# Scale part of the first mixer in column quarters between the key weights, shift part behind the query weights, dense weights packed in load order

## The chip, the core and the metric

The kernel runs on one core of one Trainium2 chip. The core has five engines with a queue of their own each: PE (TensorE: matmuls; PEld are its weight loads), DVE (VectorE), ACT (ScalarE), POOL (GpSimd) and SP, which only issues DMAs here; 16 DMA engines move data between HBM and SBUF. Each engine works through its queue in order and waits on semaphores. The metric is the device time of one execution in microseconds, less is better.

## The reference

One sequence of 256 rows of 1024, in float32. Two blocks; the first is the one that is changed:

```python
def first_block(x, c, w_in, w_out, sinks, rel_bias, w_ada, b_ada, norm_gains, w1, b1, w2, b2):
    c_act = jax.nn.silu(c)
    mod = c_act @ w_ada + b_ada                       # 1024 -> 6 x 1024
    sh1, sc1, g1, sh2, sc2, g2 = jnp.split(mod, 6, axis=-1)
    h = rmsnorm(x, norm_gains[0]) * (1.0 + sc1) + sh1
    y = token_mixer(h, w_in, w_out, sinks, bias_hb)   # h @ w_in -> qa, ka, va, qb, kb, vb
    x = x + g1 * rmsnorm(y, norm_gains[1])
    h = rmsnorm(x, norm_gains[2]) * (1.0 + sc2) + sh2
    y = jnp.square(jax.nn.relu(h @ w1 + b1)) @ w2 + b2
    return x + g2 * rmsnorm(y, norm_gains[3])
```

The mixer has 8 heads of block attention (qa, ka, va: 512 columns each) and 8 of windowed attention (qb; kb and vb of 128 columns). The second block has another mixer (mLSTM and differential attention) and a mixture of 16 experts, whose weights are most of the 511 MB that are read.

## The kernel before

Dense weights come through `Weights`. `unit` registers a load, in load order; `pump` issues the next one from SP (`dma_start` at L145) as soon as the arena (`wa` of 8 chunks of 1 MiB, `wb` of 2, `wc` of 1) has a free window; `done` frees a unit when all its readers have been issued. SP waits in order, so a load that waits for its space holds the later ones. `slice` names a part of a unit that `take` turns into two halves: a rounded high part (ACT cast, L224) and the rest as low part (DVE subtraction, L225), up to `LOOK` = 2 slices ahead. A float32 product is three matmuls, high x high, low x high and high x low (`mm3`, L304 to L306). The experts' rows come through `load_run`, into the same arenas once the dense weights have left them.

The kernel is one program; the order in which its Python emits instructions is, engine by engine, the order of the queues (`behind("x")` puts what it encloses after the instruction x). It begins with a warm-up of PE (L450), the sums of squares of X, and `sc`, silu(c) spread over 32 columns. The modulation vector is not a matmul of one row: `quarter_step` (L482) multiplies `sc` with 256 rows of a 1024-column part of `w_ada`, four matmuls of 512 columns in four groups of 32 PE columns, into one PSUM bank; after the fourth quarter `summed` (L488, L489) copies the bank and `quarter_cols` (L495, L497) sums the groups while it turns the row into a column vector `modT`, and adds the bias. That is done for the scale part (`sc0` to `sc3`), and then, between the keys, for the shift part (`sh0` to `sh3`).

X is scaled by the reciprocal of its row norm (`xn`: L695 on ACT, L696 on DVE; `rs` comes from POOL) and transposed by PE (L700) into `xT` (L703, L705). `A1` (L723, 8 columns) is the gain times one plus the scale. `key_operands` (L734 on) takes a slice of `ka` (256 rows) and makes the high and low parts of xT times A1 (`hsh` L737, `hsl` L738); `keys` (L747) multiplies. The keys are computed without the shift, whose contribution, one number a column, is added later: `shift_row` (L811) multiplies modT with the key weights, `shift_cols` (L821) turns the row, and `bk` is added when the keys leave PSUM (L856). The queries have the shift as two extra columns of `hs` instead (L772, L773; 258 columns). L762 is a small matmul that makes the distance biases (`bdist`, L764), which go out to DRAM and come back spread out as `tb`. `scaled` (L656 to L658) then makes the full normed rows `hTh`, `hTl` for the values (`va`), the second heads and so on; `acc` (L518, L520) sums a later part of `w_ada` on DVE.

Of the kernel before, what the change touches and what calls it, by code (L numbers as in the profile page):

```python
# [16 lines left out]
D = 1024  # L17
# [21 lines left out]
class Weights:  # L39
# [87 lines left out]
    def pump(self):  # L127
        while self.next < len(self.units):
            name, src, shape, row = self.units[self.next]
            n = math.prod(shape[1:])  # L130
            if row is not None:
                if not self.load_run(src, row, shape, n):
                    return
                continue
# [119 lines left out]
def block_kernel(ctx: ExitStack, tc: tile.TileContext, x, c, w_in, w_out, sinks, rel_bias, w_ada, b_ada,  # L254
                 norm_gains, w1, b1, w2, b2, norm_mix_g, w_in2, b_mgate, conv_w, conv_b, mlstm_g,
                 diff_lam, diff_g, w_up_a, w_up_b, w_out2, norm_ffn_g, w_router, w_gate_e, w_up_e,
                 w_down_e, norm_f_g, pos_hot, head_sel, out, dbg=None):
    nc = tc.nc
# [51 lines left out]
    wa = w_ada[0].rearrange("(k p) f -> p k f", p=128)  # L310
    wi = w_in[0].rearrange("(k p) f -> p k f", p=128)
    wo = w_out[0].rearrange("(k p) f -> p k f", p=128)
    w1v = w1[0].rearrange("(k p) f -> p k f", p=128)
    w2v = w2[0].rearrange("(k p) f -> p k f", p=128)
    wi2 = w_in2[0].rearrange("(k p) f -> p k f", p=128)
    wua = w_up_a[0].rearrange("(k p) f -> p k f", p=128)
    wub = w_up_b[0].rearrange("(k p) f -> p k f", p=128)
    wo2 = w_out2[0].rearrange("(k p) f -> p k f", p=128)

    def half_units(name, c0, n=2, of=None):  # L320
        w = 8 // n
        for i in of or range(n):
            W.unit(f"{name}{i}", wa[:, w * i:w * i + w, c0:c0 + 1024], [128, w, 1024], 1)

    def fm_unit(name, src, c0, n, readers=0):
        W.unit(name, src[:, :, c0:c0 + n], [128, 8, n], readers)
# [3 lines left out]
    def tm_unit(name, src, c0, n, readers=0):  # L330
        W.unit(name, src[:, :, c0:c0 + n], [128, 8, n], readers)
# [3 lines left out]
    def row_unit(name, src, k0):  # L335
        W.unit(name, src[:, k0:k0 + 4, :], [128, 4, 1024], 0)
        for k in range(4):
            W.slice(name, lambda t, k=k: t[:, k, :], [128, 1024])

    half_units("sc", 1024, 4)  # L340
    for i in range(2):
        W.unit(f"ka{i}", wi[:, 4 * i:4 * i + 4, 512:1024], [128, 4, 512], 1)
        for k in range(2):
            W.slice(f"ka{i}", lambda t, k=k: t[:, 2 * k:2 * k + 2, :], [128, 2, 512])
    W.mark("ka")
    half_units("sh", 0, 4)
    fm_unit("qa", wi, 0, 512)
    tm_unit("va", wi, 1024, 512)
    W.unit("kvb", wi[:, :, 2048:2304], [128, 8, 256], 0)
# [3 lines left out]
    W.unit("qb", wi[:, :, 1536:2048], [128, 8, 512], 0)  # L353
# [8 lines left out]
    row_unit("wo0", wo, 0)  # L362
    W.mark("wo0")
    row_unit("wo1", wo, 4)
    W.mark("w_out")
    tm_unit("w1_0", w1v, 0, 512, 1)
    W.mark("w1_0")
    for g in range(9):
        if 0 < g < 8:
            fm_unit(f"w1_{g}", w1v, g * 512, 512)  # L370
        if g > 0:
            row_unit(f"w2_{g - 1}", w2v, 4 * (g - 1))
# [3 lines left out]
    tm_unit("mv", wi2, 1024, 512)  # L376
    W.mark("mv")
    fm_unit("mk", wi2, 512, 512)
    fm_unit("mq", wi2, 0, 512)
    W.unit("mg", wi2[:, :, 2048:2064], [128, 8, 16], 1)  # L380
    tm_unit("mo", wi2, 1536, 512)
    fm_unit("dk", wi2, 2576, 512)
    fm_unit("dq", wi2, 2064, 512)
    tm_unit("dv", wi2, 3088, 512)
    for g in range(4):
        fm_unit(f"gt{g}", wi2, 3600 + g * 512, 512)
    W.mark("proj2")
    W.unit("wua", wua, [128, 4, 1024], 0)
    W.unit("wub", wub, [128, 4, 1024], 0)
# [3 lines left out]
    row_unit("wp0", wo2, 0)  # L393
    row_unit("wp1", wo2, 4)
# [15 lines left out]
    for i in range(2):  # L410
        W.unit(f"eh{i}", wde[E - 1][:, 12:16, 512 * i:512 * i + 512], [128, 4, 512], 1)
# [15 lines left out]
    hsh = sp.tile([128, 8, HW], F32R, name="hsh")  # L427
# [46 lines left out]
    def quarter_step(name, i, ps):  # L474


        t = W.raw(f"{name}{i}")
        for kk in range(2):
            k = 2 * i + kk
            for j in range(2):  # L480
                b = 64 * kk + 32 * j
                LAST["sums"] = mm(ps[b:b + 32, :], sc[:, k, :], t[:, kk, j * 512:(j + 1) * 512],  # L482
                                  start=(k < 2), stop=(k >= 6))
        W.done(f"{name}{i}")

# [196 lines left out]
    xn = big.tile([128, 2, D], F32, name="xn", tag="hTh")  # L682
# [1191 lines left out]
```

## Time and profile before

| | |
|---|---|
| three runs | 1462.71, 1465.15, 1467.64 us; median 1465.15 |
| profiled execution | 1463.22 us, its span 1461.4 us |
| PE busy | 1108.9 us (76%) |
| DVE, ACT, POOL busy | 468.4, 308.4, 156.9 us |
| HBM read | 511.41 MB, 351 GB/s over the span |
| mean DMA | 64526 packets; 46658 under 8 KB |

Busy shares are means over stages that differ: a front of some 24 us until the first key matmul, the dense stage up to about 558 us, and the experts to the end. So the rows below are read by stretch. In a timeline a row has the start, the time from the first start to the last end of such instructions in a row, the engine, the line, the operation, what is written from what, and in brackets the idle time ahead of it with what ended it. A matmul of float32 leaves two records.

### The profile page before, as it was taken

What the parts mean: (1) busy time and instruction counts of PE and PEld (TensorE: products, weight loads), DVE (VectorE), ACT (ScalarE), POOL (GpSimd) and SP (SyncE); (2) the same over time, 40 slices, a digit from 0 to 9 for tenths busy, and PEclk for the clock granted to TensorE, in tenths of its full rate; (3) what the DMA queues carried; (4) which work ended last, traced back from release to release, by engine and by line L of the source; (5) the groups of instructions that cost most, each with busy time, mean ns of one, the idle gap of its engine ahead of it and who ended that gap; (6) DMA issues with size and microseconds to landing.
All of it is one profiled execution on the core that took longest, in us unless ns stands there. A gap on an engine that the chain in (4) does not pass through costs nothing.

```text
span 1461.4 us, 16948 instructions
## 1 busy us (share of the span) xinstructions
PE 1108.9 (76%) x7140; PEld 623.7 (43%) x7140; DVE 468.4 (32%) x974; ACT 308.4 (21%) x547; POOL 156.9 (11%) x187
## 2 busy tenths in 40 slices
PE   7999999999999999857654665565656655665665
PEld 5777798988998994212111111111111111111112
DVE  4788657767888764101000010010000100001001
ACT  4555544454745541000000000000000000000001
POOL 1100534323022240000000000000000000000000
PEclk9999999999999999887788787888687879778788
DMA  9996356634438578999999999999999999999996
GB/s 365 379 345 255 121 188 248 242 138 156 150 116 317 198 322 365 430 429 432 429 430 431 430 430 432 430 430 429 430 430 428 428 433 431 431 430 429 429 430 260
DMA packets 64526, 513.58 MB, mean 351 GB/s; under 512 B 6022, under 2 KB 7239, under 8 KB 46658
## 3 DMA queue, kind: packets, MB, share of 16 engines
q1 hardware_dynamic: 62898, 508.54, 84.5%
q0 software_dynamic: 1408, 3.70, 0.8%
q8 instruction: 56, 0.92, 0.3%
q10 hardware_dynamic: 144, 0.26, 0.0%
q14 instruction: 20, 0.16, 0.0%
HBM read 511.41 MB, written 1.07 MB: 351 GB/s over the span
## 4 chain that ended last, share of the span: by engine, by line
DMA 54%; PE 40%; DVE 3%; POOL 1%; issue 1%; ACT 1%; SPq 0%; DVEq 0%; ACTq 0%; POOLq 0%
DMA we<-in_w_gate_e_dram 17%; DMA we<-in_w_up_e_dram 16%; DMA we<-in_w_down_e_dram 16%; PE tp L1683 5%; PE f L304 4%; PE f L306 4%; PE f L305 4%; PE big L304 3%; PE big L306 3%; PE big L305 3%; PE f L1701 3%; DMA wd<-in_w_down_e_dram 2%; DMA wa<-in_w_ada_dram 2%; PE tp L304 1%; PE tp L305 1%
## 5 line engine op out<-in xcount | busy, mean ns | idle before, releaser
L1683 PE MATMUL tp<-wa,work 128*32 128x512 f32 x1000 | 148.0, 745 | 102.6 <-DMA wa<-in_w_up_e_dram 79.8
L1691 DVE TENSOR_TENSOR work<-work,tp 128x512 f32<-128x512 f32 x16 | 11.0, 687 | 557.8 <-PE tp L1683 557.8
L225 DVE TENSOR_TENSOR wboth<-wa,wboth 128x1024 fp32r<-128x1024 f32 x116 | 143.8, 1246 | 44.6 <-ACT wboth L224 44.5
L224 ACT CAST wboth<-wa 128x1024 fp32r<-128x1024 f32 x116 | 120.7, 1046 | 134.6 <-PE f L306 52.5
L1683 PE MATMUL tp<-wd,work 128*32 128x512 f32 x568 | 93.1, 803 | 65.5 <-DMA wd<-in_w_gate_e_dram 36.2
L1701 PE MATMUL f<-wa,work 128*32 128x512 f32 (+1 forms) x504 | 81.6, 796 | 59.4 <-DMA wa<-in_w_down_e_dram 56.3
L1683 PEld LDWEIGHTS tp<-wa,work 128*32 128x32 f32 x1000 | 35.4, 132 | 213.2 <-DMA wa<-in_w_up_e_dram 94.1
L304 PE MATMUL f<-hTh,wboth 128*128 128x256 f32 (+1 forms) x416 | 119.4, 287 | 0.0
L1765 ACT ACTIVATE work<-f,gi 128x512 f32<-128x512 f32 x15 | 10.3, 687 | 516.5 <-PE f L1701 516.5
L306 PE MATMUL f<-hTh,wboth 128*128 128x256 f32 (+1 forms) x416 | 118.2, 284 | 0.0
L305 PE MATMUL f<-hTl,wboth 128*128 128x256 f32 (+1 forms) x416 | 117.9, 283 | 0.0
L1694 POOL TENSOR_SCALAR work<-iot,gi 128x256 f32<-128x256 f32 x16 | 14.8, 922 | 816.7 <-PE big L1769 804.7
L1766 DVE TENSOR_SCALAR work<-f,gi 128x512 f32<-128x512 f32 x15 | 11.3, 751 | 249.9 <-PE f L1701 249.9
L1683 PE MATMUL tp<-we,work 128*32 128x512 f32 x384 | 61.8, 793 | 36.2 <-DMA we<-in_w_gate_e_dram 24.9
L1683 PEld LDWEIGHTS tp<-wd,work 128*32 128x32 f32 x568 | 21.9, 143 | 135.7 <-issue 55.4
L304 PEld LDWEIGHTS f<-hTh,wboth 128*128 128x128 f32 x416 | 79.1, 190 | 1.0 <-issue 0.5
L305 PEld LDWEIGHTS f<-hTl,wboth 128*128 128x128 f32 x416 | 79.3, 191 | 0.4 <-issue 0.3
L306 PEld LDWEIGHTS f<-hTh,wboth 128*128 128x128 f32 x416 | 79.1, 190 | 0.2 <-issue 0.2
L1690 ACT ACTIVATE work<-tp 128x512 f32<-128x512 f32 x16 | 9.6, 597 | 294.6 <-PE tp L1683 294.6
L1701 PE MATMUL f<-wd,work 128*32 128x512 f32 x264 | 51.1, 859 | 26.9 <-DMA wd<-in_w_down_e_dram 26.9
L1701 PEld LDWEIGHTS f<-wa,work 128*32 128x32 f32 x504 | 22.3, 142 | 111.7 <-issue 107.6
L1769 PE MATMUL big<-work 128*128 128x512 f32 x120 | 55.1, 602 | 4.7 <-ACT work L1765 4.2
(539 smaller groups left out, 1884.1 us busy)
## 6 DMA issues: line engine op xcount, KB each, us to landing
wa<-in_w_up_e_dram SPq DMA_DIRECT2D x15, 4096.0 KB
wa<-in_w_down_e_dram SPq DMA_DIRECT2D x14, 4096.0 KB
wa<-in_w_gate_e_dram SPq DMA_DIRECT2D x14, 4096.0 KB
wa<-in_w_in_dram SPq DMA_DIRECT2D x14, 2048.0 KB
wd<-in_w_down_e_dram SPq DMA_DIRECT2D x7, 4096.0 KB
wd<-in_w_up_e_dram SPq DMA_DIRECT2D x7, 4096.0 KB
wa<-in_w_dram SPq DMA_DIRECT2D x12, 2048.0 KB
we<-in_w_gate_e_dram SPq DMA_DIRECT2D x8, 3072.0 KB
```

Source lines behind the costliest of these rows:

```text
L224: self.last = self.nc.scalar.copy(hi, src)
L225: self.last_lo = self.nc.vector.tensor_tensor(lo, src, hi.bitcast(F32), op=ALU.subtract)
L304: mm(o, a[0], b[0], start=start, stop=False)
L305: mm(o, a[0], b[1], start=False, stop=False)
L306: mm(o, a[1], b[0], start=False, stop=stop)
L1683: LAST["pe"] = mm(ps[32 * j:32 * j + 32, :], xe[:, k, :], t[:, j * 512:(j + 1) * 512], start=(k == 0), stop=(k == 7))
L1691: nc.vector.tensor_tensor(hid, hid, pu, op=ALU.mult)
L1694: nc.gpsimd.tensor_scalar(oht, iot, gi[:, 1, e:e + 1], None, op0=ALU.is_equal)
L1701: mm(ps[32 * r:32 * r + 32, :], hT[:, 4 * j + r, :], ts[r][:, a:a + n], start=(j == 0), stop=(j == 3))
L1765: nc.scalar.activation(ye[0], pd[0], AF.Copy, scale=gi[:, 0, e:e + 1])
L1766: nc.vector.tensor_scalar(ye[1], pd[1], gi[:, 0, e:e + 1], None, op0=ALU.mult)
L1769: mm(total[t][n], oht[:, t * 128:(t + 1) * 128], ye[n], start=False, stop=False)
```

## The change

The scale part is loaded as four quarters of 256 columns with all 1024 rows (`sc0` to `sc3`, 1 MiB each) that alternate with quarters of the key weights (`ka0`, `kb0`, `ka1`, `kb1`, 512 KiB each; two make one unit). `col_step` multiplies one such quarter, eight matmuls of 256 columns in four column groups, and copies the result (`mq`); `col_turn` sums and turns it, two columns of modT with two small matmuls; `scale_cols` makes two columns of A1, which is what one key slice of 256 rows needs. So each key slice has its own scale step. The shift part comes behind the query weights, as four column quarters whose steps and turns stand between the queries; the queries lose the extra columns, and get a `shift_row` and `shift_cols` of their own.

X is no longer scaled and transposed: `turn_rows` multiplies it with a diagonal matrix `dr` of the reciprocal norms (`diag`), which does both. The two warm-ups of the old turn are gone. The keys leave PSUM on DVE (four, before two on DVE and two on ACT), the queries on ACT after all four. Small loads of GpSimd go out later. All dense weights, and the last pieces of the last expert, are arranged by the host as one stream in the order and shape of the loads, so that each DMA reads one contiguous piece of DRAM.

```diff
+    def packed(key, k0, nk, c0, n):
+        nonlocal used
+        ap = flat(stream, used, [[nk * n, 128], [n, nk], [1, n]])
+        pieces.append((key, k0, nk, c0, n))
+        used += 128 * nk * n
+        return ap
...
-    half_units("sc", 1024, 4)
-    for i in range(2):
-        W.unit(f"ka{i}", wi[:, 4 * i:4 * i + 4, 512:1024], [128, 4, 512], 1)
...
+    for q in range(4):
+        W.unit(f"sc{q}", packed("w_ada", 0, 8, 1024 + 256 * q, 256), [128, 8, 256], 1)
+        rows = packed("w_in", 2 * q, 2, 512, 512)
...
-    half_units("sh", 0, 4)
-    fm_unit("qa", wi, 0, 512)
-    tm_unit("va", wi, 1024, 512)
+    fm_unit("qa", "w_in", 0, 512, 1)
+    for q in range(4):
+        W.unit(f"sh{q}", packed("w_ada", 0, 8, 256 * q, 256), [128, 8, 256], 1)
+    tm_unit("va", "w_in", 1024, 512)
...
+    def col_step(name, q):
+        t = W.raw(f"{name}{q}")
+        ps = f_ps((128, 256))
+        for k in range(8):
+            g = 32 * (k % 4)
+            LAST["sums"] = mm(ps[g:g + 32, :], sc[:, k, :], t[:, k, :], start=(k < 4), stop=(k >= 4))
+        W.done(f"{name}{q}")
+        m = mod.tile([128, 256], F32, name="mq", tag="acc", bufs=2)
+        LAST["m"] = nc.vector.tensor_copy(m, ps)
         return m
+
+    def col_turn(name, q, m):
+        ps = tp_ps((128, 2))
+        for b in range(2):
+            LAST["cols"] = mm(ps[:, b:b + 1], m[:, b * 128:(b + 1) * 128], quad, start=True, stop=True)
+        i = 8 * PARTS.index(name) + 2 * q
+        nc.vector.tensor_tensor(modT[:, i:i + 2], ps, badaT[:, i:i + 2], op=ALU.add)
...
+    def turn_rows(q):
+        for t in range(2):
+            ps = (tp_ps, f_ps)[t]((128, 4, 128))
             for i in range(4):
-                nc.tensor.transpose(ps[:, i, :], xn[:, t, (4 * q + i) * 128:(4 * q + i + 1) * 128], ident)
+                mm(ps[:, i, :], X[:, t, (4 * q + i) * 128:(4 * q + i + 1) * 128], dr[t], start=True, stop=True)
...
+    m = col_step("sc", 0)
+    turn_rows(0)
+    scale_cols(0, m)
+    turn_rows(1)
...
-    with behind("sums"):
-        warm_up(1, 256)
-    quarter_cols("sc", msc)
-    with behind("cols"):
-        warm_up(2, 256)
...
+    for k2 in range(4):
+        w = key_operands(k2)
+        keys(k2, w, ((0, 0),))
+        if k2 < 3:
+            m = col_step("sc", k2 + 1)
+        keys(k2, w, ((1, 0),))
+        if k2 < 3:
+            scale_cols(k2 + 1, m)
+        keys(k2, w, ((0, 1),))
...
+    qp = [bank((128, 2, 256)) for bank in (f_ps, tp_ps)]
+    for m in range(4):
+        fm_tile("qa", hs, qp[m // 2][:, m % 2, :])
+        col_turn("sh", m, col_step("sh", m))
     row = shift_row(["ka0", "ka1"], modT[:, 0:8], mod, "acc", 2)
...
-    queries(1)
+    rowq = shift_row(["qa"], modT[:, 0:8], mod, "acc", 2)
+    h = scaled(xT, A1, modT[:, 0:8])
```

Three places show how the queues change. The lines of the new kernel lie some 2 to 15 higher than those of the old (keys: L747 and L762; low parts: L225 and L230). `big`, `f` and `tp` are PSUM banks, `A_190` and `A_253` are A1.

**PE and DVE ahead of the keys.** PE of the kernel before, from the first transposes to the first keys:

```order
L700 MATMUL tp<-ident,xn 128x128 x4
L700 MATMUL f<-ident,xn 128x128 x2
L482 MATMUL big<-wa,sc 32x512 x4
L700 MATMUL f<-ident,xn 128x128 x4
L700 MATMUL tp<-ident,xn 128x128 x4
L482 MATMUL big<-wa,sc 32x512 x12
L450 MATMUL big<-ones_w,ones 128x256
L495 MATMUL tp<-pairs,m 128x2 x4
L450 MATMUL big<-ones_w,ones 128x256 x2
L747 MATMUL big<-hsh,wboth 128x256 x16
```

PE now:

```order
L720 MATMUL tp<-dr,X 128x128 x4
L493 MATMUL f<-wa,sc 32x256 x8
L720 MATMUL f<-dr,X 128x128 x4
L502 MATMUL tp<-quad,mq 128x1 x2
L720 MATMUL tp<-dr,X 128x128 x4
L720 MATMUL f<-dr,X 128x128 x4
L762 MATMUL big<-hsh,wboth 128x256 x8
L493 MATMUL f<-wa,sc 32x256 x8
L762 MATMUL big<-hsh,wboth 128x256 x8
L502 MATMUL tp<-quad,mq 128x1 x2
L762 MATMUL big<-hsl,wboth 128x256 x8
```

DVE now, from the copy of the first step's result to the first operands of the keys:

```order
L496 COPY mq<-f 128x256
L723 COPY xT<-f 128x4x128
L504 TENSOR_TENSOR modT<-tp,badaT 128x2
L230 TENSOR_TENSOR wboth<-wa,wboth 128x1024
L712 SCALAR_TENSOR_TENSOR A_190<-modT,nT 128x2
L723 COPY xT<-f 128x4x128
L753 SCALAR_TENSOR_TENSOR hsl<-xT,A_190,hsh 128x256 x2
```

Three of the four scale steps and their turns now stand between key matmuls. On DVE a low part (L230) stands ahead of A1.

**DVE between the keys and the queries.** Before:

```order
L738 SCALAR_TENSOR_TENSOR hsl<-xT,A_253,hsh 128x256 x2
L764 COPY bdist<-tp 16x384
L488 COPY m<-f 128x256
L489 COPY m<-f 128x256
L497 TENSOR_TENSOR modT<-tp,badaT 128x4x2
L772 CAST hsh<-modT 128x8x2
L773 TENSOR_TENSOR hsl<-modT,hsh 128x8x2
L225 TENSOR_TENSOR wboth<-wa,wboth 128x1024 x3
```

and now:

```order
L712 SCALAR_TENSOR_TENSOR A_190<-modT,nT 128x2
L753 SCALAR_TENSOR_TENSOR hsl<-xT,A_190,hsh 128x256 x2
L779 COPY bdist<-tp 16x384
L230 TENSOR_TENSOR wboth<-wa,wboth 128x1024 x3
L496 COPY mq<-f 128x256
L230 TENSOR_TENSOR wboth<-wa,wboth 128x1024
L504 TENSOR_TENSOR modT<-tp,badaT 128x2
```

The copy of the distances stands directly ahead of the low parts of the query weights; its matmul has moved behind the last keys.

**PE at the end of the shift part.** Before, where the queries begin:

```order
L482 MATMUL f<-wb,sc 32x512 x4
L747 MATMUL big<-hsl,wboth 128x256 x3
L495 MATMUL tp<-pairs,m 128x2 x4
L304 MATMUL f<-hsh,wboth 128x258
L305 MATMUL f<-hsl,wboth 128x258
L811 MATMUL f<-wa,modT 32x512
L306 MATMUL f<-hsh,wboth 128x258
```

and now, where the queries end and the values begin:

```order
L313 MATMUL tp<-hsh,wboth 128x256
L493 MATMUL f<-wa,sc 32x256 x8
L502 MATMUL tp<-quad,mq 128x1 x2
L818 MATMUL f<-wa,modT 32x512 x16
L829 MATMUL tp<-quad,row 128x1 x4
L311 MATMUL f<-wboth,hTh 128x512
L312 MATMUL f<-wboth,hTh 128x512
```

The last shift step and its turn are adjacent, both shift rows (16 matmuls) stand behind them, and the turn of the second row is among the first value matmuls.

## Rows read from the trace of the kernel before

**Rows 1.** The page's 40 slices: busy tenths, PE clock, DMA share.

```profile
PE   7999999999999999857654665565656655665665
PEclk9999999999999999887788787888687879778788
DMA  9996356634438578999999999999999999999996
```

**Rows 2.** Stretch, length, busy (count) PE, PEld, DVE, ACT, POOL; PEclk; DMA share; GB/s.

```profile
24.00:60.00 36.00, 35.15 (x266) 27.27 (x266) 23.58 (x47) 18.48 (x31) 3.55 (x5) 1.00 1.04 389
60.00:100.00 40.00, 39.85 (x279) 33.40 (x278) 36.89 (x89) 19.21 (x50) 1.54 (x2) 1.00 0.91 346
100.00:558.00 458.00, 450.68 (x2955) 394.77 (x2954) 330.94 (x663) 234.35 (x407) 130.86 (x148) 1.00 0.57 208
558.00:1447.00 889.00, 560.67 (x3520) 155.00 (x3519) 66.43 (x148) 21.46 (x34) 15.14 (x17) 0.80 1.00 428
```

**Rows 3.** The same view of the first 24 us.

```profile
8.00:10.00 2.00, 0.79 (x4) 0.54 (x5) 1.31 (x8) 1.99 (x3) 1.51 (x3) 0.62 1.02 414
10.00:14.00 4.00, 4.00 (x18) 1.81 (x19) 1.18 (x2) 2.85 (x5) 1.38 (x3) 0.50 1.03 414
16.00:24.00 8.00, 5.02 (x38) 2.20 (x30) 1.98 (x6) 1.81 (x4) 0.00 (x0) 1.00 1.04 395
```

**Rows 4.** Timeline of PE before the keys: start, duration, instruction [idle before].

```profile
11.80 1.93 PE L482 MATMUL big<-wa,sc 128*32 128x512 f32 x8
19.16 1.06 PE L482 MATMUL big<-wa,sc 128*32 128x512 f32 x8 [1.78 <-DMA wa<-in_w_ada_dram]
24.23 0.50 PE L747 MATMUL big<-hsh,wboth 128*128 128x256 f32 x2 [1.43 <-ACT wboth L224]
```

**Rows 5.** Timelines of DVE (L592 to L497) and ACT (L737) there.

```profile
6.49 0.69 DVE L592 CUSTOM_DVE_ANT_0 junk<-X 128x512 f32<-128x512 f32 x1 [5.22 <-DMA X<-in_x_dram]
9.29 0.49 DVE L696 TENSOR_SCALAR xn<-X,rs 128x512 f32<-128x512 f32 x1
10.24 0.49 DVE L696 TENSOR_SCALAR xn<-X,rs 128x512 f32<-128x512 f32 x1 [0.46 <-POOL rs L581]
20.30 0.42 DVE L488 COPY m<-big 128x256 f32<-128x256 f32 x1 [4.79 <-PE big L482]
21.86 0.17 DVE L497 TENSOR_TENSOR modT<-tp,badaT 128x8 f32<-128x8 f32 x1 [0.82 <-PE tp L495]
22.34 0.91 ACT L737 ACTIVATE hsh<-xT,A 128x256 fp32r<-128x256 f32 x2 [6.19 <-DVE A L723]
```

**Rows 6.** Timeline of PE later on; last, one piece of the chain.

```profile
41.70 1.05 PE L495 MATMUL tp<-pairs,m 128*128 128x2 f32 x8
47.60 1.92 PE L811 MATMUL f<-wa,modT 128*32 128x512 f32 x14
52.47 0.95 PE L821 MATMUL tp<-quad,row 128*128 128x1 f32 x8
561.16 1.17 PE L1672 MATMUL f<-X,hot 128*32 128x256 f32 x16
557.97 3.26 PE big L1630 x4
```

**Rows 7.** Timeline of DVE around the queries and values.

```profile
35.32 0.55 DVE L764 COPY bdist<-tp 16x384 f32<-16x384 f32 x1 [4.10 <-PE tp L762]
43.39 3.50 DVE L225 TENSOR_TENSOR wboth<-wa,wboth 128x1024 fp32r<-128x1024 f32 x3
78.13 1.28 DVE L520 SCALAR_TENSOR_TENSOR acc<-wa,sc,acc 128x1024 f32<-128x1024 f32 x1
```

**Rows 8.** DVE's load, columns as in rows 2.

```profile
60.00:70.00 10.00, 9.87 (x50) 7.33 (x49) 10.00 (x30) 5.16 (x13) 0.00 (x0) 1.00 0.98 360
```

**Rows 9.** PE's waits, 24 to 100 and 100 to 558: total, times, longest.

```profile
PE f L304 <- DVE hsh L772: 0.6, 1, 0.6
PE big L305 <- DVE wboth L225: 1.3, 1, 1.3
```

More of the change, by code (lines that the diff above doesn't have):

```diff
@@ L130, in pump @@
             n = math.prod(shape[1:])
+            if isinstance(src, tuple):
+                self.nc.sync.dma_start(self.tiles[self.names[src[0]]][:, shape[1]:], src[1])
+                self.next += 1
+                continue
             if row is not None:
@@ L309, in block_kernel @@
     W = Weights(nc, spl)
[L310 to L318, printed above, removed]
+    used = 0
+    def packed(key, k0, nk, c0, n):
[4 more added lines that the diff above has]
+        return ap
     def half_units(name, c0, n=2, of=None):
@@ L410, in block_kernel @@
     for i in range(2):
-        W.unit(f"eh{i}", wde[E - 1][:, 12:16, 512 * i:512 * i + 512], [128, 4, 512], 1)
+        W.unit(f"eh{i}", packed("last", 12, 4, 512 * i, 512), [128, 4, 512], 1)
     X = res.tile([128, 2, D], F32, name="X")
@@ L765, in block_kernel @@
         fd = dram.tile([16, 384], F32, name="fd")
-        nc.gpsimd.dma_start(fd, bdist)
-    for i in range(1, 4):
-        quarter_step("sh", i, msh)
-    keys(3, ops[3], ALL[:1])
-    quarter_cols("sh", summed(msh))
-    shift = modT[:, 0:8].rearrange("p (k o) -> p k o", o=1).to_broadcast([128, 8, 2])
-    nc.vector.tensor_copy(hs[0][:, :, S:HW], shift)
-    nc.vector.tensor_tensor(hs[1][:, :, S:HW], shift, hs[0][:, :, S:HW].bitcast(F32), op=ALU.subtract)
-    keys(3, ops[3], ALL[1:])
+        LAST["fd"] = nc.gpsimd.dma_start(fd, bdist)
     TB, LG, PTt, SP = {}, {}, {}, {}
@@ L812, in shift_row @@
                 k += 1
+        for unit in units:
             W.done(unit)
@@ L887, in proj_rest @@
         begin("gA", lambda: mod.tile([128, D], F32, name="acc", tag="acc", bufs=2))
-        begin_gate(1)
+        with behind("fd"):
+            begin_gate(1)
         for i, _ in enumerate(fm_block("qb", 4, h, put_q(4))):
@@ L1862 @@
     consts = _shape_constants()
+    src = {n: _np.asarray(inputs[n])[0].reshape(-1, 128, inputs[n].shape[-1]) for n in _STREAM}
+    src["last"] = _np.asarray(inputs["w_down_e_2"])[0, E - 1].reshape(128, 16, 1024).transpose(1, 0, 2)
+    length = sum(src[n].size for n in _STREAM) + 4 * 128 * 1024
+    stream = nc.dram_tensor("in_stream_dram", (length,), F32, kind="ExternalInput").ap()
     for name in _INS + list(consts):
@@ L1870 @@
     with _tile.TileContext(nc) as tc:
-        block_kernel(tc, *args)
+        pieces = []
+        block_kernel(tc, pieces, stream, *args)
+    arrays["in_stream_dram"] = _np.concatenate(
+        [src[n][k:k + nk, :, c:c + w].transpose(1, 0, 2).reshape(-1) for n, k, nk, c, w in pieces])
+    assert arrays["in_stream_dram"].size == length
     r = _run(nc, [arrays], core_ids=[0])
```

150 lines of the change are left out of this document (58 added, 92 removed).

## Prediction

> **What bounds the kernel now.** I read the page's slices first. PE is nearly full in slices 2 to 16, and after that it falls to five or six tenths while the DMA row stands at 9 [rows 1]. The stretches make the two regimes sharp: from 24 to 558 us the columns for PE show 35.15 of 36, 39.85 of 40 and 450.68 of 458 us busy, at a granted clock of 1.00; from 558 to 1447 us the DMA share is 1.00 at 428 GB/s [rows 2]. The second regime streams the experts' weights; what it could load early is limited by buffers that the first one releases, so I take a shift of the first regime to reach the end one for one. The question is then what the change does to PE's queue between 8 and 558 us, and nothing else.
>
> The front, up to 24 us, is different. The granted clock is 0.62 and 0.50 from 8 to 14 us, the DMA works at 395 to 414 GB/s [rows 3], and PE waits: the last scale step starts at 19.16 after 1.78 us of waiting for w_ada, and the first key matmul at 24.23 [rows 4]. Those 24 us are what the change goes after.
>
> **Part 1, the earlier start of the keys.** Now only a quarter of the scale part has to be there. I follow the longest chain. The first row scale is used at 9.29, the second at 10.24 after a wait for POOL [rows 5]; so the first diagonal matrix is ready at about 9.5. Turning rows now takes groups of four fp32 matmuls of 128 columns, full width, on which the nearest row is four of 512 columns in 3.26 us at full clock [rows 6]: 0.82 a group, 1.65 at half clock. Group one: 11.15. The first scale step has eight matmuls of 256 columns in four column groups. As many columns in 4 x 512 took 1.93 at half clock and 1.06 at full [rows 4], and eight of 256 took 1.17 elsewhere [rows 6]; with 2.1 it ends at 13.25. Group two ends at 14.9 (the 0.42 copy [rows 5] hides behind it), the turn of two columns (half of 1.05 [rows 6]) at 15.6. Then DVE: 0.17 for the add [rows 5], a low part of the key weights, which is queued ahead of A, at 1.17 (3.50 for three [rows 7]), and 0.17 for A: 17.4. ACT's first operand, 0.45 (half of 0.91 [rows 5]), and hand-overs: **keys at 18.0, a gain of 6.2 us**. If the clock is back at 13 us it is 17.1 (gain 7.1); if it stays at half until the keys, 20.0 (gain 4.2).
>
> The loads hide. X lands at 6.49 [rows 5]; at 0.4 MB/us, the level of rows 3, the first scale quarter (1.05 MB) lands at 9.1, its key rows at 10.4, the last scale quarter at 20.9 (PE wants it at about 28.6), the last key rows at 22.2, the queries at 27.5 (wanted at 36), the shift quarters at 30 to 38 (41 to 55), the values at 43 (46). In the trace the fourth piece behind X landed at 19.16 [rows 4], 2.2 us after the 17.0 that this reckoning gives it; with 2.2 more only the first quarter (11.3 for a step that can start at 11.15) would be touched, by 0.15. So I cost the packed layout and the smaller pieces at nothing; a rate a third lower puts the first quarter at 10.4, still in time.
>
> **Part 2, work that moves behind that start, onto a full PE.** Three scale steps of 1.06: +3.2. Three turns of 0.5: +1.5. The shift part has four steps as before, but four turns (2.0) in place of one of 1.05: +0.95. The queries lose their two extra columns (nothing I can see) and get a shift row of their own: eight matmuls of 512 columns, 14 records of which took 1.92 and 16 so about 2.1, and a turn of 0.95 that comes to 0.9 [rows 6]: +3.0. Together **+8.65** (7.2 if a turn is 0.3; 9.6 if a step is 1.17).
>
> **Part 3, waits.** In order:
> On DVE the copy of the bias distances (0.55) stands ahead of the low parts of the query weights (1.17) [rows 7]. The distance matmul ends the keys, and PE wants the first low part at its third query matmul, 0.25 us later: 0.06 + 0.55 + 1.17 less 0.25 is a wait of 1.6. Before, that copy was long done: the matmul stood in the middle of the keys.
> For two of the four shift quarters nothing stands between step and turn on PE, so it waits for the 0.42 copy and two hand-overs, 0.55 each: 1.1.
> Behind the queries the two shift rows share a PSUM bank with an ACT copy between them, and the values need a bank that holds queries until ACT has moved them: 0.7 and 0.8 by the order, of which I take 1.0, since ACT may be ahead.
> Of the old idle time, 0.85 us of 24 to 60 [rows 2] goes away, with it the 0.6 wait for the shift operand [rows 9]. Sum **+2.85** (0 to 4.5).
> DVE is full from 60 to 70 us, 10.00 of 10 [rows 8]. It gets the four key evacuations instead of two, and seven of the eight sums of the second shift part (1.28 each [rows 7]) now stand ahead of the copy of the second values, one more than before. Counting its queue from the softmax on, I get the low part of the second query weights 1.2 us after PE wants it: **+1.2** (0 to 3).
> Further on little can be won back: in 100 to 558 us PE waits for a weight's low part once, for 1.3 us [rows 9], and if late weights stand behind that, packed rows shorten it. I take half, **-0.7**, with 0 and -1.3 as bounds.
>
> **Sum.** -6.2 + 8.65 + 2.85 + 1.2 - 0.7 = +5.8 us. The profiled execution took 1463.22 us, so it would become 1469.0; it stands 1.9 under the median of the runs, 1465.15, on which the same 5.8 gives **1471.0**.
>
> **Rivals.** (a) *Slack swallows the waits, no change.* If DVE and ACT run ahead, Part 3's first two sums go to zero or below, and with a start at 17.1 the rest is -7.1 + 7.2 + 0 to 0.5 - 0.7: about -0.3, 1465. It needs the low parts of the queries made before the distance copy, which the order on DVE speaks against, and turns at 0.3. With half of it, +2.5: 1467.6.
> (b) *The stream paces the dense phase, faster.* If PE's busy rows hide matmuls stretched by late weights, packed rows at 428 GB/s in place of 389 [rows 2] bring the weights of the first 60 us some 5 us earlier (a tenth of 52 us), and the start of 18.0 counts as well: 1458 to 1460. It decides only where PE ends a wait on a load; between 24 and 100 us its one wait of the trace is on DVE [rows 9]. Little chance.
> (c) *The clock stays low into the keys, slower still.* The trace has 0.50 while PE worked 4.00 of 4 us, and 1.00 only from 16 us on [rows 3]; the two warm-ups around the old turn are gone. Start at 20.0 and the first key block of 3 us dearer by as much as 1.5: +9.3, 1474.4.
> The Trainium skill ("TensorE: Matmul & The Clock Gate", "HAM oscillation") says that a PE that waits between groups of matmuls drops to half clock and begins the next group cold. The trace agrees for 8 to 14 us; by that rule, applied to the gaps that the new chain has at 14 to 18 us, the time would be that of (c).
> (d) *DVE's queue grows.* If each wait feeds the next, the 1.2 of Part 3 becomes 4: 1473.8.
>
> **How the numbers follow.** Forecast (+3.5 to +7.5) 0.52; (a) 0.26; (b) 0.06; (c) 0.08; (d) 0.08. About 0.3%, 4.4 us, is what a measurement of this kernel can tell from no change. Faster by more: (b), 0.06. Slower by more: (c), (d) and four fifths of the forecast, 0.58. The rest, 0.36, is the same. The range leaves out (b), a little of (a), and what lies over (c) and (d) together: 1462 to 1476.5.
>
> **What would show it.** Right: first key matmul near 18; steps near 1.1 and turns near 0.5 between key matmuls without waits; PE waiting about 1.6 on DVE's low part at the third query matmul; the first value matmul some 4 us later than before; waits for DVE near 90 us; experts' stream later by the same shift. Wrong: a start before 17 or after 20; a PE that waits for a load in the keys or queries (then the packing matters); a dense phase whose shift shrinks between 100 and 558 us, which would mean slack that I did not see; an end that doesn't follow the dense phase.

## The result and the profile after

The changed kernel takes **1480.09 us** (median of four runs, 1478.15 to 1482.97); the kernel before, measured beside it, 1465.93 (1462.71 to 1467.64). The ratio is 1.0099, its 95% interval 1.0080 to 1.0117: 14.2 us slower. The forecast was 5.8 slower, with an upper end of 1476.5: the direction is right, the size is not.

The profiled execution of after took 1482.97 us (span 1481.2) and is the longest of its four; that of before, 1463.22, is shorter than its median. So the two traces lie 19.8 us apart and the medians 14.2. I take *places* from the traces and *sizes* from the medians where both exist.

The DMA share in the 40 slices of the page of after, to be held against [rows 1]:

```profile
DMA  9787256544537489899999999999999999999995
```

In the first slices DMA now has 7, 8, 7, 2, where it had 9, 9, 6, 3, and slice 17 has an 8 in place of a 9. The stretches of after, with the columns of [rows 2]; they answer to the first lines of [rows 2, 3]:

```profile
8.00:10.00 2.00, 1.33 (x7) 1.07 (x7) 0.90 (x7) 1.97 (x3) 1.26 (x3) 0.50 1.00 397
10.00:14.00 4.00, 4.00 (x26) 2.51 (x26) 0.59 (x2) 2.33 (x4) 2.21 (x4) 0.50 1.02 426
24.00:60.00 36.00, 33.27 (x293) 26.05 (x282) 19.07 (x41) 12.11 (x18) 2.60 (x4) 0.95 0.86 339
60.00:100.00 40.00, 37.98 (x267) 31.03 (x268) 34.72 (x76) 20.15 (x47) 2.24 (x3) 1.00 0.86 340
100.00:558.00 458.00, 448.60 (x2931) 391.07 (x2930) 332.67 (x664) 232.48 (x406) 130.85 (x147) 0.99 0.55 205
```

PE, which had 0.85 and 0.15 us idle from 24 to 60 and from 60 to 100, now has 2.73 and 2.02, and the DMA share of the first of these fell from 1.04 to 0.86. The timeline of PE in after, read as [rows 4, 6]:

```profile
11.15 1.94 PE L493 MATMUL f<-wa,sc 128*32 128x256 f32 x16
17.55 1.20 PE L762 MATMUL big<-hsh,wboth 128*128 128x256 f32 x8 [0.42 <-ACT hsh L752]
18.68 1.07 PE L493 MATMUL f<-wa,sc 128*32 128x256 f32 x16
20.73 0.50 PE L502 MATMUL tp<-quad,mq 128*128 128x1 f32 x4
37.30 0.39 PE L313 MATMUL f<-hsh,wboth 128*128 128x256 f32 x1 [1.34 <-DVE wboth L230]
60.43 1.92 PE L818 MATMUL f<-wa,modT 128*32 128x512 f32 x16 [0.71 <-ACT row L823]
66.25 0.93 PE L923 MATMUL big<-kT,qT 64*128 64x128 f32 x8
101.70 0.92 PE L923 MATMUL f<-kT,qT 64*128 64x128 f32 x4
115.08 3.78 PE L577 MATMUL f<-acc,ones 128*128 128x512 f32 x4 [3.16 <-DVE acc L534]
118.80 2.67 PE L545 MATMUL f<-wa,sc 128*32 128x512 f32 x16
576.64 1.06 PE L1685 MATMUL tp<-wd,work 128*32 128x512 f32 x8 [0.76 <-PE tp L1712]
```

In before, the first scores, the first scores that go into bank `f`, and the first expert matmul:

```profile
59.27 0.93 PE L921 MATMUL big<-kT,qT 64*128 64x128 f32 x8
95.33 0.92 PE L921 MATMUL f<-kT,qT 64*128 64x128 f32 x4
563.42 1.07 PE L1683 MATMUL tp<-wd,work 128*32 128x512 f32 x8 [0.77 <-PE tp L1710]
```

The keys start 6.7 us earlier (24.23 to 17.55), the first expert matmul comes 13.2 later, the end 19.8 later. The first scores stand 7.0 later, but they are not at the same place of PE's queue: in after eight of the first 24 value matmuls stand ahead of them, in before none. Where PE has the same work behind it in both kernels, the shift is smaller: 5.0 at the second group of scores (66.02 to 71.01), 6.4 at the first scores in bank `f` (95.33 to 101.70), which I call *the mark*. There are thus two surprises: 6.8 us between the mark and the first expert matmul, and 6.6 behind the first expert matmul, where the two kernels issue the same work. I call the time from the first expert matmul to the end of the span the *experts' stage*; it is 898.0 us in before and 904.6 in after.

PE's waits in after (total us, times, longest), 24 to 100 us and then two of those from 100 to 575, to be held against [rows 9]:

```profile
PE f L313 <- DVE wboth L230: 2.0, 2, 1.3
PE tp L502 <- DVE mq L496: 1.1, 2, 0.5
PE f L311 <- ACT vT L871: 0.9, 1, 0.9
PE f L818 <- ACT row L823: 0.7, 1, 0.7
```

```profile
PE f L577 <- DVE acc L534: 3.2, 1, 3.2
PE big L312 <- DVE wboth L230: 1.3, 1, 1.3
```

Three of the first four are those of the prediction's Part 3 (the 2.0 is 1.34 at the third query matmul and 0.67 near 88 us). The 0.9 is another one: at 80.05 us PE waits for a bank until ACT has copied the first values (L871). The 3.2 us for the sum of a gate's modulation (L577 needs `acc`, which DVE sums over pieces of `w_ada`) is new; before had no such wait.

### The profile page after: what moved, and what is told of

It is laid out like the page before. It is cut to its first block, busy times and chain, and to the rows that moved or that the text cites. A ratio compares the mean times of both kernels' runs of the same rounds, so it can differ in the third digit from the quotient of the medians.

```text
span 1481.2 us, 17197 instructions
## 1 busy us (share of the span) xinstructions
PE 1116.5 (75%) x7254; PEld 630.9 (43%) x7254; DVE 472.1 (32%) x984; ACT 307.4 (21%) x544; POOL 157.1 (11%) x187
## 2 busy tenths in 40 slices
DMA packets 32159, 513.60 MB, mean 347 GB/s; under 512 B 5014, under 2 KB 5335, under 8 KB 7378
## 3 DMA queue, kind: packets, MB, share of 16 engines
HBM read 511.41 MB, written 1.07 MB: 346 GB/s over the span
## 4 chain that ended last, share of the span: by engine, by line
DMA 52%; PE 39%; DVE 4%; POOL 2%; issue 1%; ACT 1%; DVEq 0%; SPq 0%; ACTq 0%; POOLq 0%
DMA we<-in_w_down_e_dram 18%; DMA we<-in_w_gate_e_dram 17%; DMA we<-in_w_up_e_dram 16%; PE tp L1685 5%; PE f L311 3%; PE f L313 3%; PE f L312 3%; PE big L311 3%; PE big L313 3%; PE big L312 3%; PE f L1703 3%; PE tp L311 1%; PE tp L313 1%; PE tp L312 1%; PE big L762 1%
## 5 line engine op out<-in xcount | busy, mean ns | idle before, releaser
L1685 PE MATMUL tp<-wa,work 128*32 128x512 f32 x984 | 156.1, 791 | 97.1 <-DMA wa<-in_w_up_e_dram 55.8
L230 DVE TENSOR_TENSOR wboth<-wa,wboth 128x1024 fp32r<-128x1024 f32 x116 | 143.7, 1246 | 43.9 <-ACT wboth L229 43.9
L312 PE MATMUL f<-hTl,wboth 128*128 128x256 f32 (+1 forms) x416 | 117.8, 283 | 0.0
L1703 PE MATMUL f<-wa,work 128*32 128x512 f32 (+1 forms) x504 | 74.6, 736 | 46.7 <-DMA wa<-in_w_down_e_dram 44.7
L312 PEld LDWEIGHTS f<-hTl,wboth 128*128 128x128 f32 x416 | 79.4, 191 | 0.1
```

Of the source, the lines that this page charges most:

```text
L230: self.last_lo = self.nc.vector.tensor_tensor(lo, src, hi.bitcast(F32), op=ALU.subtract)
L312: mm(o, a[0], b[1], start=False, stop=False)
L1685: LAST["pe"] = mm(ps[32 * j:32 * j + 32, :], xe[:, k, :], t[:, j * 512:(j + 1) * 512], start=(k == 0), stop=(k == 7))
L1703: mm(ps[32 * r:32 * r + 32, :], hT[:, 4 * j + r, :], ts[r][:, a:a + n], start=(j == 0), stop=(j == 3))
```

## The experiments

All ratios are to the kernel before on the same chip, with 95% intervals.

### Which part of the change it is

The packed stream alone, in the kernel before (*pack_only*; one of the loads, the others alike):

```diff
...
-        W.unit(name, src[:, :, c0:c0 + n], [128, 8, n], readers)
+        W.unit(name, packed(src, 0, 8, c0, n), [128, 8, n], readers)
...
```

> The kernel before with only the packed stream: same loads, same order, same compute, but each dense DMA reads one contiguous piece. Theory 1 (the loss is made on PE, DVE and by buffers that come free late, all of it in the new order of the front): within 2 us of the kernel before, at most 1 us faster, since PE waits for almost no load between 24 and 558 us. Rival (the packed layout itself is slower or disturbs the experts' stream): 5 to 14 us slower.

1464.10 us (10 runs), ratio 0.9991 [0.9980, 1.0003]: no change that can be measured. And the reverse, the changed kernel with the weights read from their own arrays (*after_unpacked*):

```diff
...
-        ap = flat(stream, used, [[nk * n, 128], [n, nk], [1, n]])
...
+        return originals[key][0].rearrange("(k p) f -> p k f", p=128)[:, k0:k0 + nk, c0:c0 + n]
...
```

> The changed kernel with its order, but every dense load read from the original tensors, as before the change (quarters of 256 columns in rows of 1 KB, halves of 512 columns in rows of 2 KB). Theory 1: as slow as the changed kernel, 1478 to 1483 us; if rows of 1 KB land later than the keys want them, up to 3 us more. Rival (packing is the loss): back within 4 us of the kernel before.

1480.44, ratio 1.0099 [1.0062, 1.0136], the ratio of after. So packing is worth nothing that can be measured, either way, though it halves the DMA packets (64526 in before, 32015 in *pack_only*, 70559 in *after_unpacked*, 32159 in after). Then the two halves of the reordering, each with packed weights; the edits are against *pack_only*. The scale part early, the shift part as it was (*scale_only*):

```diff
-    half_units("sc", 1024, 4)
...
+    for q in range(4):
+        W.unit(f"sc{q}", packed("w_ada", 0, 8, 1024 + 256 * q, 256), [128, 8, 256], 1)
+        rows = packed("w_in", 2 * q, 2, 512, 512)
...
     half_units("sh", 0, 4)
     fm_unit("qa", "w_in", 0, 512)
...
```

> Packed stream, new scale part (quarters between the keys, rows turned with the diagonal matrix), but the shift part as before: four row quarters between the keys, loaded ahead of the query weights, two extra columns in the queries, one shift row. Theory 1 says the shift part makes the loss: first key matmul at 17.6 (6.7 us earlier), 4.7 us of scale steps and turns behind it, so about 2 us faster than before (0 to 3), first scores about 57 us, no DMA pause at 54 to 59 us, no half-clock stretch at 112 to 120 us. Rival (the early scale part makes the loss): 6 us or more slower than before.

1468.52 (10 runs), ratio 1.0022 [1.0007, 1.0037]. Its first scores stand at 57.01 us, 2.3 before those of before, and its first expert matmul at 561.96, 1.5 before; yet it is slower. Its experts' stage has 902.6 us. The shift part behind the queries, the scale part as it was (*shift_only*):

```diff
     half_units("sc", 1024, 4)
...
-    half_units("sh", 0, 4)
-    fm_unit("qa", "w_in", 0, 512)
+    fm_unit("qa", "w_in", 0, 512, 1)
+    for q in range(4):
+        W.unit(f"sh{q}", packed("w_ada", 0, 8, 256 * q, 256), [128, 8, 256], 1)
...
```

> Packed stream, scale part as before (row quarters, all ahead of the keys), and the new shift part alone: column quarters behind the query weights, steps and turns between the queries, a shift row for the queries. Theory 1: keys start at 24 us, and the whole loss of the change is here, 13 to 17 us slower than before, with PE waiting for the gate sum of DVE around 115 to 120 us and a half-clock stretch behind it. Rival (the early scale part makes the loss): within 5 us of before.

1477.19, ratio 1.0083 [1.0056, 1.0110]: this half brings most of the loss. Its first expert matmul is at 571.02, 7.6 later than before's, and its experts' stage 903.1. Both halves have the longer experts' stage, and so has after: the two losses, 3.2 and 11.8 us against before on their chip, hold that stage twice and are not parts of a sum.

### Where the dense stage loses

In after, SP's wait for the shift rows (total, times, longest; 20 to 125 us), and a stretch in which it falls (columns of [rows 2]):

```profile
SPq L150 <- PE f L818: 14.2, 2, 11.2
```

```profile
54.00:60.00 6.00, 5.18 (x51) 2.87 (x49) 3.60 (x10) 2.81 (x5) 0.00 (x0) 1.00 0.13 30
```

The key and query weights are held until the two shift rows have read them, at 57.8 to 62.3 us; SP stands on a load that needs their space, and DMA moves 30 GB/s. My idea was that this pause makes the pieces of `w_ada` late, and with them DVE's sums and the gate. To try it without the hold, both shift rows read the value weights, which arrive later and are free later anyway (*rows_from_values*; the keys and queries then get a wrong shift, and the counts of readers follow):

```diff
...
-    row = shift_row(["ka0", "ka1"], modT[:, 0:8], mod, "acc", 2)
-    rowq = shift_row(["qa"], modT[:, 0:8], mod, "acc", 2)
+    row = shift_row(["va"], modT[:, 0:8], mod, "acc", 2)
+    rowq = shift_row(["va"], modT[:, 0:8], mod, "acc", 2)
...
```

> The changed kernel, but both shift rows multiply the shift with the value weights instead of the key and query weights (the output is wrong by that: keys and queries get the wrong shift): the same matmuls on PE, but the key and query buffers come free when their weights have been split, not behind the two shift rows. Theory 1 (buffers held by the shift rows stop the loads at 54 to 59 us, the sums on DVE come late, PE waits 3.2 us for the gate sum at 112 to 115 us and then runs at half clock): no pause of the DMA at 54 to 59 us, the wait at 112 us under 1 us, 4 to 6 us faster than the changed kernel, near 1475. Rival (DVE's own queue makes it late: evacuations, low parts, the order of the sums): loads earlier, but the wait and the time unchanged within 1.5 us.

1473.58 (10 runs), ratio 1.0048 [1.0030, 1.0066]. The same stretch in this kernel, one further on, and its gate matmul:

```profile
54.00:60.00 6.00, 4.75 (x49) 2.26 (x51) 3.66 (x7) 3.41 (x5) 0.00 (x0) 1.00 1.01 422
118.00:130.00 12.00, 12.00 (x44) 8.00 (x44) 6.95 (x21) 5.18 (x13) 0.00 (x0) 0.57 0.88 373
```

```profile
111.91 1.98 PE L577 MATMUL f<-acc,ones 128*128 128x512 f32 x4 [0.80 <-DVE acc L534]
```

The pause is gone (422 GB/s) and the wait fell from 3.16 to 0.80: the chain from the held buffers to the gate is shown. But in this execution the granted clock then fell to 0.57 from 118 to 130 us, with PE at 12.00 of 12, and the first expert matmul stands at 575.63, only 1.0 earlier than in after, though the gate's matmul is 3.2 earlier. The gain of this kernel lies behind it: its experts' stage has 897.6 us, like before's.

The wait at the third query matmul is taken away by computing the distance biases between the keys again:

```diff
-    with behind("keys"):
...
+        if k2 == 2:
+            with behind("keys"):
...
```

> The changed kernel with the small distance matmul and its copy behind the third key slice instead of behind all keys. Theory 1: the wait of 1.3 us at the third query matmul goes, and with it the half-clock stretch at 38 to 41.5 us that costs 1.7: 3.0 us faster up to the first scores (63.3 us), and 2 to 4 us faster at the end. Rival (the slack is lost again further on, because DVE is late there): first scores 3 us earlier, end within 1 us of the changed kernel.

1478.69, ratio 1.0080 [1.0057, 1.0104]. In another kernel the wait stays, but PE is given three matmuls ahead of it whose result nobody reads:

```diff
+        pw = tp_ps()
+        for _ in range(3):
+            mm(pw[:, 0:256], ones, ones_w[:, 0:256], start=True, stop=True)
```

> The changed kernel with three idle matmuls of 256 columns (0.43 us each) behind the distance matmul, in the 1.3 us in which PE waits there. If the half clock that follows comes from that wait: granted clock 1.00 from 36 to 42 us, first scores 1.5 us earlier, end 1 to 2 us faster. Rival (the clock falls for another reason): clock as before, first scores no earlier, up to 0.3 us later.

1479.51, ratio 1.0096 [1.0067, 1.0125]. The stretch of the first query matmuls (columns of [rows 2]) in after, in the kernel with early distances, and in the one with three more matmuls, in this order:

```profile
36.00:42.00 6.00, 4.70 (x30) 4.21 (x34) 3.52 (x4) 0.50 (x1) 1.06 (x2) 0.72 1.00 421
```

```profile
36.00:42.00 6.00, 6.00 (x59) 5.28 (x59) 3.91 (x7) 2.54 (x3) 1.54 (x2) 1.00 1.02 429
```

```profile
36.00:42.00 6.00, 5.96 (x56) 5.01 (x55) 4.31 (x6) 1.04 (x1) 1.30 (x3) 1.00 1.01 425
```

From the first key matmul to the first scores after takes 48.7 us, the filled kernel 47.1, the one with early distances 45.4. So the wait of 1.3 cost 3.3 there, about half of it by the clock that fell behind it (0.72 in these six us) and that three matmuls hold up. At the end little of it shows: against the kernel before on their chip these two are 13.5 and 14.3 us slower, after 14.2, which is within the spread of the runs.

The same for the gate, 14 unread matmuls ahead of L577's place:

```diff
+            if g == 1 and j == 0:
+                for _ in range(14):
+                    mm(ps[:, 0:128], ones, ones, start=True, stop=True)
```

> The changed kernel with 14 idle matmuls of 128 columns (3.0 us) on PE right ahead of the gate matmul that waits 3.2 us for DVE. If the half-clock stretch from 113 to 121 us comes from that wait: granted clock 1.00 there, dense stage 2.5 to 3 us shorter behind it, end 2 to 3 us earlier. Rival (the clock falls there for what PE does around it, column-group and 64-row matmuls, as it did with hardly a wait when the shift rows read the value weights): still half clock, no gain.

1481.48, ratio 1.0106 [1.0087, 1.0125]. The clock is 1.00 from 106 to 130 us and the four gate matmuls take 1.98 us in place of 3.78. From the first scores to the first expert matmul it takes 509.6 us, after 510.4, before 504.2, but this says little of what the clock costs at the gate: in this execution it fell elsewhere, ahead of the unread matmuls and with PE busy throughout, where after had 1.00.

```profile
94.00:98.00 4.00, 4.00 (x23) 4.00 (x23) 3.80 (x10) 1.67 (x8) 0.00 (x0) 0.58 1.00 410
```

The price is seen better in a kernel of the next part (*after_placed*) that has the same wait and kept its clock. From the mark to the turn behind the gate, in before, after and that kernel, in this order (columns of [rows 2]):

```profile
95.33:110.28 14.95, 14.78 (x104) 8.04 (x103) 12.46 (x41) 9.49 (x27) 0.75 (x1) 1.00 1.02 392
```

```profile
101.70:122.38 20.68, 16.57 (x103) 8.50 (x103) 15.94 (x45) 9.49 (x27) 0.79 (x1) 0.83 0.76 286
```

```profile
100.85:118.99 18.14, 14.03 (x103) 7.91 (x103) 15.84 (x45) 9.52 (x27) 0.79 (x1) 1.00 0.75 267
```

After takes 5.7 us longer here than before. PE's idle time is 3.9 longer, of which the gate's wait is 3.16, and PE is busy for 2.5 us more than in the kernel that kept 1.00 (16.57 against 14.03; before has the same work in another order, 14.78). So the wait and the clock behind it make most of the 6.8 us; from there to the first expert matmul after takes 1.1 us longer than before.

### Why the experts' stage is longer

In the experts' stage SP issues the same loads, but they go to the places that are free. A load of an expert's `w_up` in after, in before, and what SP waits for there (timeline of SP: start, duration; then its waits from 555 to 625 in after, 540 to 620 in before):

```profile
585.48 24.63 SPq L182 DMA_DIRECT2D wd<-in_w_up_e_dram  x3
610.16 0.42 SPq L182 DMA_DIRECT2D wa<-in_w_up_e_dram  x1
```

```profile
SPq L182 <- PE tp L1685: 34.1, 12, 19.5
```

```profile
572.26 2.75 SPq L177 DMA_DIRECT2D wd<-in_w_up_e_dram  x2
587.53 0.33 SPq L177 DMA_DIRECT2D wa<-in_w_up_e_dram  x1
```

```profile
SPq L177 <- PE tp L1683: 24.6, 11, 11.6
```

Before issues two loads of 1 MiB into `wd`, then one of 4 MiB into `wa` (and a last one of 1 MiB into `wd`). After issues three into `wd`, of which the third has 3 MiB, and 2 MiB into `wa`; the third waits 19.5 us until PE has left that space, with every later load behind it. In before no such wait is longer than 11.6. Five us, from 21 us after that load's issue on, in after, and the same five in before (columns of [rows 2]):

```profile
606.64:611.64 5.00, 5.00 (x39) 1.39 (x41) 0.00 (x0) 0.00 (x0) 0.92 (x1) 1.00 0.30 82
```

```profile
593.42:598.42 5.00, 5.00 (x39) 1.38 (x41) 0.00 (x0) 0.00 (x0) 0.92 (x1) 1.00 1.01 433
```

DMA, which sets the pace here (a share of 1.00 over the stage in before [rows 2]), pauses. Which chunks are free at 580 us hangs on which were taken and freed since the first load: `wa` has eight chunks, and the first six pieces now arrive, and are freed, in another order. Three kernels test that by giving only these first six pieces other chunks. The changed kernel, with keys in chunks 2 and 3 and the scale quarters around them (*after_placed*):

```diff
+    PIN = {'sc0': 0, 'sc1': 1, 'ka0': 2, 'ka1': 3, 'sc2': 4, 'sc3': 5}
...
+            if name in self.PIN:
+                a, c = self.arenas[0], self.PIN[name]
+                w = (a, c) if all(x is None for x in a[1][c:c + m]) else None
```

> The changed kernel with the first six pieces put into other places of the arena (first two scale quarters in chunks 0 and 1, keys in 2 and 3, the other scale quarters in 4 and 5); PE, DVE and ACT have the same order, but the experts' loads then fall into the same pieces as in the kernel before (a run of 8192 columns in one place instead of 6144 in one and 4096 in another). Theory (the place of the dense loads decides which expert load waits 19 us for its space, and the DMA pauses for some 5 us at 607 to 612): pause gone, 4 to 6 us faster than the changed kernel, near 1475. Rival (the experts' stage is longer for another reason): within 1.5 us of the changed kernel.

1473.00, ratio 1.0056 [1.0038, 1.0073]: 7.7 us slower than before on its chip, where after is 14.2 slower. That is 6.4 us less, by six numbers. Next, the kernel with the early scale part alone, given the chunks that the kernel before uses (scale 0 to 3, keys 4 and 5; *scale_placed*):

```diff
+    PIN = {'sc0': 0, 'sc1': 1, 'sc2': 2, 'sc3': 3, 'ka0': 4, 'ka1': 5}
```

> The kernel with the early scale part and the old shift part, its first six pieces in the places of the kernel before. Its dense stage ended 1.5 us earlier than before, and its experts' stage took 4.6 us longer. Theory (place): that 4.6 goes, so 1 to 3 us faster than the kernel before, near 1463. Rival: as scale_only, 3 us slower than before.

1462.66 (12 runs), ratio 0.9986 [0.9976, 0.9996]: 2.6 us faster than before on its chip, where unplaced it is 3.2 slower. Some of the 2.6 may be the packed stream, which alone gave 0.9991. Last, the kernel before itself, with the chunks changed and nothing else (*before_misplaced*):

```diff
+    PIN = {'sc0': 0, 'sc1': 1, 'ka0': 2, 'ka1': 3, 'sc2': 4, 'sc3': 5}
```

> The kernel before, with nothing changed but the places of its first six pieces in the arena (scale quarters in chunks 0, 1, 4, 5, keys in 2 and 3): orders of PE, DVE and ACT as before, dense weights not packed, but the experts' loads fall into the pieces that they have in the changed kernel (6144 and 4096 columns instead of 8192 and 2048). Theory (place): a load of w_up waits some 19 us for its space, the DMA pauses some 5 us about 30 us behind the dense stage, 4 to 7 us slower than before, 1469.5 to 1472. Rival (the pause needs the changed order or the packed stream): within 1.5 us of before.

1470.35 (12 runs), ratio 1.0031 [1.0019, 1.0044]: 4.9 us slower. The load in question in the placed changed kernel and in the misplaced kernel before, and SP's wait in the latter:

```profile
582.85 2.23 SPq L187 DMA_DIRECT2D wd<-in_w_up_e_dram  x2
596.42 0.33 SPq L187 DMA_DIRECT2D wa<-in_w_up_e_dram  x1
```

```profile
576.71 24.48 SPq L182 DMA_DIRECT2D wd<-in_w_up_e_dram  x3
601.24 0.42 SPq L182 DMA_DIRECT2D wa<-in_w_up_e_dram  x1
```

```profile
SPq L182 <- PE tp L1688: 36.2, 13, 19.2
```

The same five us in the misplaced kernel, from 21 us after the load's issue on:

```profile
598.00:603.00 5.00, 5.00 (x43) 1.44 (x45) 0.00 (x0) 0.00 (x0) 0.92 (x1) 1.00 0.31 82
```

The misplaced kernel has after's long wait and after's pause (0.31, 82 GB/s), while the placed one has before's order, two into `wd` and then `wa`. All profiles put side by side (us; worked out from the span and the start of the first expert matmul):

| kernel | median | first expert matmul | experts' stage |
|---|---|---|---|
| before | 1465.93 | 563.42 | 898.0 |
| pack_only | 1464.10 | 562.64 | 897.6 |
| scale_placed | 1462.66 | 566.17 | 897.8 |
| after_placed | 1473.00 | 574.01 | 896.7 |
| rows_from_values | 1473.58 | 575.63 | 897.6 |
| scale_placed_warm (below) | 1462.78 | 562.31 | 897.6 |
| filler | 1479.51 | 574.64 | 901.1 |
| scale_only | 1468.52 | 561.96 | 902.6 |
| dist_early | 1478.69 | 573.79 | 902.9 |
| shift_only | 1477.19 | 571.02 | 903.1 |
| before_misplaced | 1470.35 | 567.71 | 903.0 |
| after_unpacked | 1480.44 | 575.37 | 903.3 |
| fill_gate | 1481.48 | 575.02 | 904.4 |
| after | 1480.09 | 576.64 | 904.6 |

Apart from the filler the experts' stage has two lengths, some 897 and some 903 to 905 us, and which of them a kernel has does not go by when its dense stage ends. (The profiles are single executions, so rows differ by a few us in the middle column: the misplaced kernel's execution has its keys at 25.48, and a clock of 0.50 from 24 to 30 us.)

### A version that beats both

The early scale part with the old places, and a warm-up of PE that reaches up to the first real matmul:

```diff
-    warm_up(12, 128)
+    warm_up(18, 128)
```

> scale_placed with 18 instead of 12 warm-up matmuls at the start, to bridge the 2 us in which PE waits for the identity before 8 us. If that gap is what drops the clock to 0.50 from 8 to 14 us: clock 1.00 there, the turning of the rows and the first step 3 us shorter, keys up to 2 us earlier if the first scale quarter has landed (it then decides), 1 to 2 us faster than scale_placed. Rival (the chain is sparse anyway, or waits for the load): within 0.5 us of scale_placed, or slower where the six matmuls delay the first transposes.

1462.78 us (12 runs), ratio 0.9980 [0.9967, 0.9993]. Stretch 10 to 12 us (columns of [rows 2]) in *scale_placed* and in this kernel:

```profile
10.00:12.00 2.00, 2.00 (x12) 1.59 (x15) 0.28 (x1) 1.55 (x3) 2.00 (x4) 0.50 1.00 420
```

```profile
10.00:12.00 2.00, 2.00 (x26) 1.30 (x25) 0.41 (x2) 1.99 (x4) 2.00 (x4) 1.00 1.00 414
```

In these profiles the clock of the front went from 0.50 to 1.00 and the first key matmul from 18.22 to 15.55. By the medians (1462.66 and 1462.78) the two versions can't be told apart; they are 2.6 and 2.5 us faster than the kernel before, less than 0.2%.

## Why the prediction was wrong

**The failed step is the first paragraph's "a shift of the first regime to reach the end one for one".** It took the experts' stage as a stream that starts earlier or later and is otherwise the same. It isn't: the change of load order moves where its loads land, and one landing place costs a pause of the resource that sets the pace. By medians that is 6.4 us of the 14.2 (after and after_placed, each against before on its chip), and 4.9 and 5.8 in the two other pairs. Without it the change costs 7.7 us (1473.00 against 1465.26), inside the range given. The reasoning went by queues and durations, not by places.

**The second failed step is Part 3's last paragraph, "Further on little can be won back".** It put the time behind the mark at -0.7 us. In the traces it is +6.8: the gate's wait of 3.16 at L577, a clock of 0.83 around it, and other waits below 1 us. I counted how long the shift rows take, but not that the buffers that they read are held so long; Part 1's "The loads hide" looked forward to 46 us and stopped there. The saving of 0.7 by earlier weights did not come: L312 waits 1.3 as before.

**Part 1 held.** Keys at 18.0 predicted, 17.55 measured, with the clock at 0.50 from 8 to 14 us. In other executions of nearly the same front the clock was 0.72 there and the keys came at 16.7 (17.1 was given for an early return). No load was waited for.

**Up to the mark the sum held, in part by luck.** Without the -0.7 it gives +6.5, and +6.4 was measured. The stretch from the first key matmul to the mark in before, in after, and in the kernel with early distances, whose clock stayed at 1.00 (columns of [rows 2]):

```profile
24.23:95.33 71.10, 70.33 (x508) 56.97 (x508) 56.19 (x116) 34.84 (x69) 4.35 (x6) 1.00 0.97 363
```

```profile
17.55:101.70 84.15, 79.40 (x631) 63.85 (x631) 57.80 (x126) 35.39 (x69) 4.84 (x7) 0.98 0.88 349
```

```profile
18.05:98.89 80.84, 77.45 (x632) 62.46 (x632) 57.79 (x126) 35.41 (x69) 4.84 (x7) 1.00 0.90 359
```

*Part 2* was too dear: the work that moved behind the start is +7.1 us of busy time (70.33 to 77.45), not +8.65, though steps of 1.07, turns of 0.50 and a shift row of 1.92 are as forecast. The terms were lengths of rows, and rows in a queue overlap: the step at 18.68 has its follower at 19.68. (The upper value of 9.6 for a dearer step should be 9.4 at most.) *Part 3* held in sum: idle time rose by 4.0 us (0.77 to 4.75), and 4.05 were forecast. The wait at the third query matmul has 1.34 (forecast 1.6, though its terms add to 1.5), the shift turns 1.1 (1.1), the bank of the two shift rows 0.7, the low part near 90 us 0.7 (1.2). The values did not wait for the bank of the queries; a wait of 0.9 for the bank of the values came instead. What was missing is the price of the clock behind the 1.34, 2.0 us (79.40 to 77.45) or 1.6 by the filled kernel. So work that was 1.5 too dear made up for a clock that was not in the sum.

**The rivals.** (a) and (b) fall: the waits were there, no load is waited for in the keys, and packing moves nothing. (c) falls as it was put, since the keys ran at full clock; the low clock came later, behind the waits at 36 and 112 us. The Trainium skill's rule that it drew on ("TensorE: Matmul & The Clock Gate", "HAM oscillation") fits those two places of after, and not the placed kernel, where the same wait of 3.18 was followed by a clock of 1.00. (d) had the right engine, DVE, late by 3.2, but the cause is late loads, not a longer queue.

**What stays open.** From the turn behind the gate to the first expert matmul before takes 453.1 us and after 454.3, but the kernel with only the shift part moved 457.6 and the one whose shift rows read the values 458.9. Part of that is clock (0.57 from 116 to 120 us in the first, from 118 to 130 in the second); I did not separate the remainder. Nor do the runs tell how the 7.7 us of the placed kernel divide between the waits and the clock by medians: the clock differs from execution to execution, and each kernel has one trace.

## What to carry to other kernels

Where loads take the first free space, a change of their order at the start is a change of every place after it: compare which buffer each late load gets, and what it then waits for, before taking a shift as one for one. A buffer that gets a further reader late in the program holds up the queue that fills it; look for who needs what is queued behind, here a sum of a gate 50 us later. And when a part of a change wins in its own stretch but loses at the end, as the early scale part did, the two can be parted: pinning six chunks turned +3.2 us into -2.6.

## What the runs showed of the chip

The granted clock did not follow from PE's waits alone. In after it was 0.72 from 36 to 42 us behind a wait of 1.34, and 0.66 from 112 to 122 behind one of 3.16; the placed kernel, with the same work and the same wait, had 0.72 at the first place too, but kept 1.00 at the second (its stretch from 100.85 us is shown above; here after's, then the placed kernel's row of PE's timeline):

```profile
112.00:122.00 10.00, 6.92 (x24) 2.21 (x24) 6.17 (x15) 4.65 (x12) 0.00 (x0) 0.66 0.70 256
```

```profile
114.25 1.98 PE L582 MATMUL f<-acc,ones 128*128 128x512 f32 x4 [3.18 <-DVE acc L539]
```

And in the kernel whose shift rows read the values it fell to 0.57 from 118 to 130 us though PE had work in 12.00 of 12 and the last wait ahead was 0.80; in the kernel with the filled gate to 0.58 from 94 to 98 us with PE busy in 4.00 of 4, where after, with the same work up to there, had 1.00. What decides it these runs don't tell. The other surprise is that half as many, longer DMA packets (32015 for 64526) changed the time by less than 0.3%.
